# First weight slabs in four pieces with the squares held to their order, the last branch product moved behind the gate tiles, and own areas for the last two tiles

## The chip, the cores and the metric

The kernel runs on one core of one Trainium2 chip. The metric is the device time of one execution in microseconds (us). Numbers of the trace come from one profiled execution, counted from its first instruction.

## The reference, cut to what matters

One step of a decoder layer is computed for 512 prompt tokens and 8 times 4 sample tokens, 544 in all, in float32.

```
n = RMSNorm(h);  z = n @ W_in            # q | k | v | gate | u | v2 | gA | gB
branch A: retention per head (4 heads) -> group RMS norm -> * silu(gate)
branch B: gv = LayerNorm(gelu(v2));  yB = gelu(u) * (W_s[g] gv + b[g])
h += (sigmoid(gA) * (yA @ W_br_a) + sigmoid(gB) * (yB @ W_br_b)) @ W_o
h += relu(RMSNorm(h) @ W_up)^2 @ W_down
h += sigmoid(RMSNorm(h) @ W_pg) * (p @ W_pp)
y = RMSNorm(h)
```

W_s is lower triangular in chunks of 128 tokens. Outputs besides y are the retention states and the layer norm's result for the sample tokens.

## The kernel before, in words

Activations lie transposed: a tile is 128 features by 544 tokens, in one of 62 (later 69, then 74) **slots**, taken with `get()` from a first-in-first-out list and given back with `put()`. Each float32 operand is split into a high and a low part: `split` rounds on ScalarE (ACT, L124) and takes the rest on VectorE (DVE, L125). A product is three matmuls (high-high, high-low, low-high) on each half of 272 tokens, so one 128x128 block of weights costs six matmuls and one output tile over 1024 features 48 (`tile_of`, `dense`, L290). Large later products use a scheme with seven block products instead of eight (`fast_run`, L376).

**Feed.** Weights come in slabs of 128x1024 float32 (512 KB). `Feed.load` issues their DMAs on SyncE's queue (SP) into few raw buffers; `fill` splits them into few `hl` buffers ahead of use; `take` hands one over. For the fast scheme some sums of slabs are made by an accumulating DMA on GpSimd's queue (POOL) and on DVE (L226, L227).

**Order.** Python traces the instructions in program order; `later(n, fn)` and `chores` put work n ticks ahead, and `dense` ticks every second block. A scheduler with a simulated clock then orders each engine's queue: an instruction whose operands look ready may go ahead of earlier ones that wait. On the chip every queue runs in that fixed order. `pin`, which the change uses, ties an instruction behind the one traced before it on its engine.

**Start.** L544 to L555 load the eight input tiles x0 to x7; each is scaled and split (`scaled_split`, L481 on ACT, L482 on DVE). The first two slabs (both columns of q of head 0) come in two pieces each, slab 0 behind x0 and slab 1 behind x4. `first_two` then runs both q tiles block by block. `start_norm` squares the eight tiles (L454, L457), adds them up (L458), and `inverse_rms` sums over features with a matmul of ones (L470), then root (L473, ACT) and reciprocal (L475, DVE). `normalise` (L607), `times_r1` (L584) and `rotary` on DVE need that reciprocal.

**Middle.** Behind head 3 come the eight tiles of the gMLP's v2, m = 0 to 7 (`tiles_in`, gelu on ACT, L969; then transposed by `gated_by_token`, L956 to L962). Between m = 3 and m = 4 the PSUM pools are changed and `branch_a(3)` runs (eight products, added to the sum on DVE, L643). `x_operands` makes the operands of the fast scheme (L980 and L318 to L327) in four chores. In the run that follows, in the fast scheme (gelu of u, the gelu run), chores make the statistics (L1018), the `moments` (root on ACT, L1024, which needs another function table than gelu) and the `layer_norm` (ten DVE instructions, L1054). Tiny ACT copies (`after`, L990) hold back the loads of `wst`, `bs` and `wss`, the spatial weights. `spatial` (L1086 to L1107) runs in the next such run, that of sigmoid(gA).

**End.** The last stage runs half by half of the tokens: `gate_tiles` gives two W_pg tiles of 272 tokens one PSUM area (`two_banks`, one tile in each bank), which is read at L1320, or, for the very last pair, one tile at a time at L1326: times the norm's factor, sigmoid (L1327), times the embedding (L1330), added to h (L1331), squared (L1333, L1335). The very last tile goes in two pieces of 136 tokens. L1329 is a tiny root that fetches ACT's root table early. `finish` then makes the last norm (L470, L473, L475), scales (L1370, L1373) and stores.

Of the kernel before, what the change touches and what calls it, by code (L numbers as in the profile page):

```python
# [9 lines left out]
F32R = mybir.dt.float32r  # L10
# [4 lines left out]
P = 128  # L15
# [23 lines left out]
FIRST = (0, 4)  # L39
# [48 lines left out]
def layer(tc, a, o):  # L88
    nc = tc.nc
    act, dve, pool, pe = nc.scalar, nc.vector, nc.gpsimd, nc.tensor  # L90
    with ExitStack() as ctx:
# [35 lines left out]
        class Feed:  # L127
# [26 lines left out]
            def load(self, pieces=1):  # L154
                while self.jobs:
# [12 lines left out]
                    for i in range(pieces):  # L168
                        c = slice(i * SLAB // pieces, (i + 1) * SLAB // pieces)
                        nc.sync.dma_start(t[:, c], srcs[0][:, c])  # L170
                    self.loaded.append((kind, [t]))
                    if pieces > 1:
                        return
# [18 lines left out]
            def wide(self, src, pieces=1):  # L192
                pool_, n = self.hl_turn[0]
                self.hl_turn.rotate(-1)
                t = pool_.tile([P, 2 * SLAB], F32R, tag="hl", name="hl", bufs=n)
                for i in range(pieces):
                    c, d = (slice(i * SLAB // pieces + e, (i + 1) * SLAB // pieces + e) for e in (0, SLAB))
                    split(t[:, c], t[:, d], src[:, c])
                return [(t[:, :SLAB], t[:, SLAB:])]
# [14 lines left out]
            def expand(self, kind, tiles):  # L214
# [23 lines left out]
                return [("wide", lambda: done(self.wide(tiles[0], 2 if kind == "halves" else 1), 1))]  # L238
# [213 lines left out]
        def add_square(total, src, first):  # L452
            if first:
                act.activation(total, src, AF.Square)  # L454
            else:
                t = get()
                act.activation(t, src, AF.Square)  # L457
                dve.tensor_tensor(out=total, in0=total, in1=t, op=ALU.add)  # L458
                put(t)
# [31 lines left out]
        for h in range(H):  # L491
            for i in range(12):
                feed.plan("halves" if h == 0 and i < 2 else "plain", a["w_in"][12 * h + i])
# [49 lines left out]

        xs_raw, xs = [], []  # L544
        for k in range(KD):
# [25 lines left out]
        def start_norm():  # L571
            total = get()
            for k in range(KD):
                add_square(total, xs_raw[k], k == 0)
# [413 lines left out]
        def after(t, x):  # L988

            act.copy(t[:1, :1], x[:1, :1])  # L990

        def spatial_weights(x):
            after(wst[:, 0], x)
            nc.sync.dma_start(wst, a["wsT"])
# [5 lines left out]
        def sample_weights(x):  # L1000
            after(bs[:, 0], x)
            nc.sync.dma_start(bs, a["bs"])
            after(wss[:, 0, 0], x)
            nc.sync.dma_start(wss, a["wsS"])
# [9 lines left out]
        def statistics(i):  # L1014

            for j in range(5):
                n = P if j < 4 else NS
                dve.bn_stats(out=stats[:n, j, i], in_=gvt[j][i][:n, :512])  # L1018

        def moments():  # L1020
# [3 lines left out]
            act.activation(mv[:, :, 1], mv[:, :, 1], AF.Sqrt, bias=eps, scale=1.0)  # L1024
            dve.reciprocal(mv[:, :, 1], mv[:, :, 1])

        for m in range(0, KD, 2):
            if m == 4:
# [14 lines left out]
                branch_a(before.h, before.ya)  # L1043
                chores([(1 + 4 * k, x_operands, k) for k in range(4)])
            for i, t in enumerate(tiles_in(AF.Gelu)):
                later(2 * i + 2, lambda m=m + i, t=t: gated_by_token(m, t))
            if m == 4:
                later(2, lambda: statistics(0))

        def layer_norm(j):  # L1050
            n = P if j < 4 else NS
            for i in range(2):
                x = gvt[j][i][:n, :512]
                dve.tensor_scalar(  # L1054
                    out=x, in0=x, scalar1=mv[:n, j, 0:1], scalar2=mv[:n, j, 1:2], op0=ALU.subtract, op1=ALU.mult
                )
# [11 lines left out]

        us = []
        chores([(7, statistics, 1), (9, moments)] + [(12 + 3 * j, layer_norm, j) for j in range(5)])  # L1070
        later(26, sample_gates)
        for u2 in fast_run([(x_ops, AF.Gelu)] * 4):
# [412 lines left out]
```

## Time and profile before

| | us |
|---|---|
| median of 3 runs | 1270.65 (1269.56 to 1272.1) |
| the profiled execution's own time | 1270.25 |
| its span from first to last instruction | 1268.3 |
| TensorE busy in it | 1241.2 (98%) |
| DVE, ACT, GpSimd busy | 886.2, 625.4, 92.8 |

The 1.95 us between the span and the execution's own time lie outside what the trace records. Busy time of TensorE is modelled from the starts of pipelined matmuls, so a busy TensorE can still run slowly; how many matmuls a stretch holds tells more.

### The profile page before, as it was taken

The page shows a single profiled execution, that of the slowest core. Times are in us where ns is not written, and L with a number is a line of the kernel's source. Part 1 is how long each engine was busy: PE and PEld are TensorE (multiplying, and loading weights), DVE is VectorE, ACT ScalarE, POOL GpSimd, SP SyncE. Part 2 cuts the span into 40 slices and gives each one's busy share as a digit, 9 for nine tenths or more (in the row PEclk, how much of TensorE's full clock was granted, in tenths as well). Part 3 has the DMA queues.
Part 4 walks back from the last instruction along what each step waited for, and adds up shares of the span by engine and source line. Part 5 has one row for each costly group of instructions (what it writes and reads, how often), then busy time and mean ns, then how long its engine had stood idle before and what let it go on. Part 6 is the DMA issues. An engine that isn't in the chain of part 4 may idle for free.

```text
span 1268.3 us, 22931 instructions
## 1 busy us (share of the span) xinstructions
PE 1241.2 (98%) x9432; PEld 1209.1 (95%) x9432; DVE 886.2 (70%) x1293; ACT 625.4 (49%) x1044; POOL 92.8 (7%) x127
## 2 busy tenths in 40 slices
PE   9999999999999999999899999999999999999995
PEld 8989999999999998999899999999999999999995
DVE  7976853696468645864778654559359889878966
ACT  6454553344434443623545532445248558577732
POOL 0211100110010001000110000000000000000000
PEclk9999999999999999999999999999999999999998
DMA  8228223722273226543654552223546667755302
GB/s 323 98 99 272 98 83 112 277 82 88 98 261 106 67 92 221 172 137 78 188 142 127 158 202 93 89 79 99 118 125 159 173 164 186 186 153 146 117 18 71
DMA packets 64760, 176.27 MB, mean 139 GB/s; under 512 B 7344, under 2 KB 9648, under 8 KB 64656
## 3 DMA queue, kind: packets, MB, share of 16 engines
q1 hardware_dynamic: 53712, 135.42, 32.1%
q0 software_dynamic: 10944, 39.39, 13.3%
q8 instruction: 74, 1.21, 0.4%
q14 instruction: 30, 0.25, 0.1%
HBM read 153.55 MB, written 21.23 MB: 138 GB/s over the span
## 4 chain that ended last, share of the span: by engine, by line
PE 90%; DVE 5%; ACT 2%; DMA 1%; issue 1%; POOL 0%; SPq 0%; DVEq 0%; ACTq 0%
PE f L290 48%; PE fa L376 15%; PE f L376 11%; PE pg L290 4%; PE o L450 2%; PE st L450 2%; DVE hl L125 2%; PE sc L450 1%; PE su L813 1%; PE so L810 1%; PE so L811 1%; ACT hl L124 1%; DVE s L125 1%; PE norm L470 1%; PE sp L1086 1%
## 5 line engine op out<-in xcount | busy, mean ns | idle before, releaser
L290 PE MATMUL f<-s,hl 128*128 128x272 f32 x5088 | 674.6, 290 | 3.7 <-DVE s L482 0.9
L290 PEld LDWEIGHTS f<-s,hl 128*128 128x128 f32 x5088 | 655.4, 188 | 12.2 <-DVE s L482 1.6
L125 DVE TENSOR_TENSOR hl<-raw,hl 128x1024 fp32r<-128x1024 f32 (+1 forms) x255 | 288.4, 1138 | 114.3 <-ACT hl L124 110.9
L124 ACT CAST hl<-raw 128x1024 fp32r<-128x1024 f32 (+1 forms) x255 | 248.3, 980 | 179.3 <-PE f L290 108.5
L376 PE MATMUL fa<-s,hl 128*128 128x272 f32 x1728 | 241.3, 290 | 5.4 <-ACT hl L124 4.3
L376 PEld LDWEIGHTS fa<-s,hl 128*128 128x128 f32 x1728 | 225.2, 189 | 8.2 <-ACT hl L124 5.2
L376 PE MATMUL f<-s,hl 128*128 128x272 f32 x1296 | 184.7, 290 | 2.9 <-DVE s L395 1.1
L376 PEld LDWEIGHTS f<-s,hl 128*128 128x128 f32 x1296 | 171.1, 189 | 4.8 <-DVE s L395 2.0
L124 ACT CAST s<-s 128x544 fp32r<-128x544 f32 (+4 forms) x170 | 97.2, 597 | 51.9 <-DVE s L319 12.5
L125 DVE TENSOR_TENSOR s<-s,s 128x544 fp32r<-128x544 f32 (+4 forms) x170 | 108.0, 656 | 6.2 <-ACT s L124 5.6
L814 DVE SCALAR_TENSOR_TENSOR state<-state,su 128x512 f32<-128x512 f32 x64 | 43.6, 684 | 37.8 <-PE su L813 37.7
L125 DVE TENSOR_TENSOR s<-state,s 128x512 fp32r<-128x512 f32 x64 | 42.7, 686 | 20.2 <-ACT s L124 17.2
L124 ACT CAST s<-state 128x512 fp32r<-128x512 f32 x64 | 37.8, 620 | 38.5 <-DMA state<-in_state 20.0
L403 ACT ACTIVATE s<-fa 128x272 f32<-128x272 f32 x36 | 14.3, 397 | 62.1 <-PE fa L376 62.1
L590 ACT COPY s<-f 128x544 f32<-128x544 f32 x28 | 17.2, 614 | 50.1 <-PE f L290 50.0
L475 DVE RECIPROCAL s<-s 128x544 f32<-128x544 f32 (+1 forms) x9 | 28.6, 3173 | 9.6 <-ACT s L473 9.6
L180 POOL DMA_DIRECT2D raw<-in_w_up x12 | 10.4, 864 | 306.8 <-DVE s L125 186.8
L643 DVE TENSOR_TENSOR s<-s,f 128x544 f32<-128x544 f32 x24 | 17.2, 716 | 19.8 <-PE f L290 19.8
L290 PE MATMUL pg<-s,s 128*128 128x272 f32 x240 | 30.7, 288 | 0.0
L290 PEld LDWEIGHTS pg<-s,s 128*128 128x128 f32 x240 | 30.3, 188 | 0.1
L818 POOL DMA_DIRECT2D out_state_s<-state x32 | 22.9, 716 | 101.0 <-DVE state L814 101.0
L450 PE MATMUL o<-s,vh 128*128 128x256 f32 (+2 forms) x128 | 30.3, 323 | 0.0
(183 smaller groups left out, 1125.0 us busy)
## 6 DMA issues: line engine op xcount, KB each, us to landing
raw<-in_w_in SPq DMA_DIRECT2D x66, 512.0 KB, 3.3
state<-in_state SPq DMA_DIRECT2D x32, 512.0 KB, 4.7
out_state_s<-state POOLq DMA_DIRECT2D x32, 512.0 KB, 4.5
raw<-in_w_in SPq DMA_DIRECT2D x40, 256.0 KB, 3.2
raw<-in_w_up SPq DMA_DIRECT2D x20, 512.0 KB, 3.3
raw<-in_w_down SPq DMA_DIRECT2D x20, 512.0 KB, 3.3
raw<-in_w_up SPq DMA_DIRECT2D x36, 256.0 KB, 3.1
raw<-in_w_down SPq DMA_DIRECT2D x36, 256.0 KB, 3.3
```

The costliest lines, as they stand in the source:

```text
L124: act.copy(hi, src)
L125: dve.tensor_tensor(out=lo, in0=src, in1=hi.bitcast(F32), op=ALU.subtract)
L290: pe.matmul(ps.p[s], w, x[:, s * TH : (s + 1) * TH], start=first and i == 0 and j == 0, stop=last and i == n - 1 and j == 2, skip_group_ch ...
L376: pe.matmul(ps, a_, b_, start=first and k == j == 0, stop=k == 3 and j == 2, skip_group_check=True)
L403: act.activation(t1[:, hi_half], pa, AF.Copy, scale=-1.0)
L450: pe.matmul(ps[:rows, c], u, v, start=i == 0 and j == 0, stop=i == n - 1 and j == 2)
L470: pe.matmul(ps, ones, t[:, c0 - at0 : c1 - at0], start=i == 0, stop=i == len(totals) - 1)
L475: dve.reciprocal(r[:, c], r[:, c])
L590: act.copy(halves(t), ps.all)
L643: dve.tensor_tensor(out=halves(acc_a[m]), in0=halves(acc_a[m]), in1=ps.all, op=ALU.add)
L814: dve.scalar_tensor_tensor(out=raw[:, i], in0=raw[:, i], scalar=gamma**LS, in1=ps, op0=ALU.mult, op1=ALU.add)
L818: pool.dma_start(o["state_s"][b, c.h].rearrange("(i p) v -> p i v", i=2), raw)
```

## The change

**At the start** both first slabs are begun together and come in four pieces of 256 columns (128 KB each), a piece of both behind x0, x2, x4 and x6, split as they come. The squares and their sum are traced behind that loop and pinned there.

**In the middle** all eight v2 tiles come ahead of `branch_a(3)`, whose slabs are also loaded later. The first statistics are spread over the tiles m = 6 and 7, the second ones, the moments and the layer norm over `branch_a(3)`, pinned in the order of tracing. The loads of the spatial weights are pinned on SP behind what was traced there, in place of the ACT copies. `spatial` runs two at a time behind each pair of the gelu run.

**At the end** the last two tiles of the second half get an area of two banks each, and L1326 reads the second tile from its own.

```
+        feed.begin(2)
...
-            if k in FIRST:
-                feed.load(2)
-            if k == 1:
-                feed.fill(1)
-            if k == FIRST[1] + 1:
-                feed.fill(2)
+            if k % 2 == 0:
+                feed.piece(k // 2)
+        total = get()
+        for k in range(KD):
+            add_square(total, xs_raw[k], k == 0, pin)
...
+            def begin(self, n):
+                self.first = []
+                for _ in range(n):
+                    _, srcs = self.jobs.popleft()
+                    hl = self.hl()
+                    self.first.append((self.raw(), hl, srcs[0]))
+                    self.parts.append(("wide", [(hl[:, :SLAB], hl[:, SLAB:])]))
+            def piece(self, i):
+                c, d = (slice(i * SLAB // 4 + e, (i + 1) * SLAB // 4 + e) for e in (0, SLAB))
+                for t, hl, src in self.first:
+                    nc.sync.dma_start(t[:, c], src[:, c])
+                for t, hl, src in self.first:
+                    split(hl[:, c], hl[:, d], t[:, c])
...
         for i in range(48, 56):
             feed.plan("plain", a["w_in"][i])
-            if i == 51:
-                plan_branch_a(H - 1)
+        plan_branch_a(H - 1)
...
-                branch_a(before.h, before.ya)
                 chores([(1 + 4 * k, x_operands, k) for k in range(4)])
+                spatial_weights()
...
             if m == 4:
-                later(2, lambda: statistics(0))
+                chores([(3 + 2 * j, statistics, 0, j) for j in range(5)])
...
-        chores([(7, statistics, 1), (9, moments)] + [(12 + 3 * j, layer_norm, j) for j in range(5)])
-        later(26, sample_gates)
+        sample_weights()
+        chores([(5 + j // 2, statistics, 1, j) for j in range(5)] + [(8, moments)])
+        chores([(9 + j, layer_norm, j) for j in range(5)])
+        branch_a(before.h, before.ya)
+        later(6, sample_gates)
+        us = []
         for u2 in fast_run([(x_ops, AF.Gelu)] * 4):
             us += u2
-            if len(us) == 2:
-                spatial_weights(us[0])
-            if len(us) == 4:
-                sample_weights(us[2])
+            chores([(1 + 3 * i, spatial, len(us) - 2 + i) for i in range(2)])
-        chores([(1 + 3 * m, spatial, m) for m in range(KD)])
...
+                elif s and i == KD - 2:
+                    todo = [*gate_tiles(s, ms[:1]), *gate_tiles(s, ms[1:])]
...
-                            dve.tensor_tensor(out=t1[:, p], in0=area[:, j, p], in1=r3[:, c], op=ALU.mult)
+                            ps = todo[0] if j else area
+                            dve.tensor_tensor(out=t1[:, p], in0=ps[:, 0, p], in1=r3[:, c], op=ALU.mult)
```

## Rows read from the trace of the kernel before

**Rows 1.** The page: busy us of each engine (share of the span) and instructions, then the shares of the span along the chain that ended last.
```profile
PE 1241.2 (98%) x9432; PEld 1209.1 (95%) x9432; DVE 886.2 (70%) x1293; ACT 625.4 (49%) x1044; POOL 92.8 (7%) x127
PE 90%; DVE 5%; ACT 2%; DMA 1%; issue 1%; POOL 0%; SPq 0%; DVEq 0%; ACTq 0%
```

**Rows 2.** Busy time by stretch: from:to, its us, then busy us (and instructions) of PE, PEld, DVE, ACT and POOL, the granted TensorE clock (1.00 is full), the DMA engines' share, GB/s.
```profile
22.90:60.00 37.10, 35.98 (x283) 35.11 (x281) 36.30 (x49) 18.23 (x29) 7.79 (x7) 1.00 0.44 164
845.00:925.00 80.00, 80.00 (x637) 79.96 (x636) 56.66 (x81) 34.69 (x50) 2.59 (x3) 1.00 0.38 106
```

**Rows 3.** The chain that ended last, in order of time, in the first 62 us: start, us, what.
```profile
2.67 4.96 DMA s<-in_xT
...
12.52 0.52 ACT hl L124
...
13.08 9.23 PE f L290 x70
22.31 0.93 PE norm L470 x4
...
24.89 1.22 DVE hl L125
26.11 3.48 DVE s L475
...
51.37 0.65 DVE s L584
```

**Rows 4.** Groups by line and shape in the first 23 us: busy us, mean ns of one, and the idle time before them with what ended it.
```profile
L482 DVE SCALAR_TENSOR_TENSOR s<-s,gcols,s 128x544 fp32r<-128x544 f32 x8 | 6.2, 781 | 4.1 <-ACT s L481 4.0
L481 ACT ACTIVATE s<-s,gcols 128x544 fp32r<-128x544 f32 x8 | 5.9, 740 | 2.0 <-DMA s<-in_xT 2.0
L458 DVE TENSOR_TENSOR s<-s,s 128x544 f32<-128x544 f32 x7 | 5.0, 719 | 0.0
L457 ACT ACTIVATE s<-s 128x544 f32<-128x544 f32 x7 | 4.5, 643 | 0.0
L125 DVE TENSOR_TENSOR hl<-raw,hl 128x512 fp32r<-128x512 f32 x4 | 2.7, 688 | 1.1 <-ACT hl L124 1.1
L124 ACT CAST hl<-raw 128x512 fp32r<-128x512 f32 x4 | 2.3, 610 | 0.9 <-DMA raw<-in_w_in 0.9
L124 ACT CAST hl<-raw 128x1024 fp32r<-128x1024 f32 x2 | 2.1, 1048 | 2.7 <-DMA raw<-in_w_in 2.7
L125 DVE TENSOR_TENSOR hl<-raw,hl 128x1024 fp32r<-128x1024 f32 x1 | 1.2, 1224 | 1.9 <-ACT hl L124 1.9
```

**Rows 5.** SyncE's queue in the first 60 us: two of its waits (us in total, times, longest), then three of its issues in order of time.
```profile
SPq L565 <- DMA s<-in_xT: 1.1, 3, 0.4
SPq L170 <- DMA s<-in_sin: 0.3, 1, 0.3
...
8.37 0.33 SPq L557 DMA_DIRECT2D s<-in_cos  x1
...
13.29 0.45 SPq L653 DMA_DIRECT2D dtab<-in_dtab  x1
...
14.76 1.29 SPq L170 DMA_DIRECT2D raw<-in_w_in  x3
```

**Rows 6.** The timeline of ACT, DVE and PE from 19 to 23 us: start, us, engine, line, what, and in brackets the idle time before and what ended it.
```profile
19.85 1.05 ACT L124 CAST hl<-raw 128x1024 fp32r<-128x1024 f32 x1 [2.73 <-DMA raw<-in_w_in]
20.93 1.22 DVE L125 TENSOR_TENSOR hl<-raw,hl 128x1024 fp32r<-128x1024 f32 x1 [1.88 <-ACT hl L124]
...
22.86 18.48 PE L290 MATMUL f<-s,hl 128*128 128x272 f32 x144
```

**Rows 7.** The timeline around the moments and the layer norm (columns as in rows 6).
```profile
602.90 1.28 ACT L1024 ACT_TABLE_LOAD   x1
...
604.75 4.64 DVE L1054 TENSOR_SCALAR s<-s,mv 128x512 f32<-128x512 f32 x10
...
606.39 1.28 ACT L414 ACT_TABLE_LOAD   x1
...
609.59 0.52 PE L376 MATMUL fa<-s,hl 128*128 128x272 f32 x2 [2.64 <-ACT hl L124]
...
610.59 2.28 PE L376 MATMUL fa<-s,hl 128*128 128x272 f32 x10 [0.47 <-DVE hl L125]
```

**Rows 8.** Busy time by stretch (columns as in rows 2): `branch_a(3)`, the tiles m = 4 to 7, the stall, two pieces of it, and a stretch with `spatial`.
```profile
538.60:563.80 25.20, 25.20 (x201) 25.18 (x202) 16.93 (x24) 6.89 (x16) 2.85 (x4) 1.00 0.50 126
563.80:589.10 25.30, 25.30 (x204) 25.28 (x203) 11.26 (x15) 8.50 (x19) 0.86 (x1) 1.00 0.41 122
605.40:614.90 9.50, 5.96 (x30) 5.21 (x29) 9.50 (x16) 5.34 (x9) 1.09 (x1) 0.82 0.66 151
609.50:610.60 1.10, 0.54 (x3) 0.32 (x3) 1.10 (x2) 0.04 (x1) 0.00 (x0) 1.00 0.76 104
611.50:612.50 1.00, 1.00 (x7) 1.00 (x6) 1.00 (x2) 0.60 (x2) 0.00 (x0) 0.50 1.02 234
625.00:674.00 49.00, 49.00 (x385) 48.00 (x384) 35.18 (x51) 23.76 (x39) 6.32 (x6) 1.00 0.65 165
```

**Rows 9.** The timeline where the PSUM pools change, and one line's instructions (ns least, median, most; first and last start).
```profile
538.58 3.28 PE L290 MATMUL f<-s,hl 128*128 128x272 f32 x24 [0.71 <-ACT s L969]
...
L980 DVE SCALAR_TENSOR_TENSOR s<-s,gcols,s x8: 776/785/786, 507.3 to 567.0; 128x544 f32<-128x544 f32 x8
```

**Rows 10.** The timeline of the end (columns as in rows 6).
```profile
1233.45 1.09 PE L470 MATMUL norm<-s,ones 128*128 128x136 f32 x8
...
1252.59 0.85 DVE L1326 TENSOR_TENSOR s<-pg,s 128x272 f32<-128x272 f32 x3 [1.34 <-PE pg L290]
1253.06 0.84 ACT L1327 ACTIVATE s<-s 128x272 f32<-128x272 f32 x3 [2.64 <-DVE s L1326]
...
1253.92 1.28 ACT L1329 ACT_TABLE_LOAD   x1
...
1255.45 0.30 DVE L1330 TENSOR_TENSOR s<-s,s 128x136 f32<-128x136 f32 x1 [0.92 <-ACT warm L1329]
1255.67 0.50 DVE L1331 TENSOR_TENSOR s<-s,s 128x136 f32<-128x136 f32 x2
...
1256.30 0.43 DVE L1346 TENSOR_TENSOR s<-s,s 128x272 f32<-128x272 f32 x1
...
1256.88 2.15 PE L470 MATMUL norm<-s,ones 128*128 128x136 f32 x8 [4.33 <-DVE s L1346]
```

More of the change, by code (lines that the diff above doesn't have):

```diff
@@ L38 @@
 WARM = 12
-FIRST = (0, 4)
 QK = ((7, 8, 9, 10), (0, 2, 4, 7))
@@ L152, in raw, with load @@
                 return pool_.tile([P, SLAB], F32, tag="raw", name="raw", bufs=n)
-            def load(self, pieces=1):
+            def begin(self, n):
[11 more added lines that the diff above has]
+                    split(hl[:, c], hl[:, d], t[:, c])
+                if i == 3:
+                    self.busy -= len(self.first)
+            def load(self):
                 while self.jobs:
@@ L167, in load @@
                     t = self.raw()
-                    for i in range(pieces):
-                        c = slice(i * SLAB // pieces, (i + 1) * SLAB // pieces)
-                        nc.sync.dma_start(t[:, c], srcs[0][:, c])
+                    nc.sync.dma_start(t, srcs[0])
                     self.loaded.append((kind, [t]))
-                    if pieces > 1:
-                        return
             def load_sums(self, s0, s1):
@@ L190, in load_pair, with hl, wide @@
                 return v, t, w
-            def wide(self, src, pieces=1):
+            def hl(self):
                 pool_, n = self.hl_turn[0]
                 self.hl_turn.rotate(-1)
[L195 to L198, printed above, removed]
+                return pool_.tile([P, 2 * SLAB], F32R, tag="hl", name="hl", bufs=n)
+            def wide(self, src):
+                t = self.hl()
+                split(t[:, :SLAB], t[:, SLAB:], src)
                 return [(t[:, :SLAB], t[:, SLAB:])]
@@ L237, in expand @@
                     return [("slots", lambda: done(self.stay(tiles[0]), 1))]
-                return [("wide", lambda: done(self.wide(tiles[0], 2 if kind == "halves" else 1), 1))]
+                return [("wide", lambda: done(self.wide(tiles[0]), 1))]
             def fill(self, n, **held):
@@ L492, in layer @@
             for i in range(12):
-                feed.plan("halves" if h == 0 and i < 2 else "plain", a["w_in"][12 * h + i])
+                feed.plan("plain", a["w_in"][12 * h + i])
                 if h and i == 3:
@@ L986, in x_operands, with spatial_weights @@
                 put(r1s["r"])
[L988 to L994, printed above, removed]
+        def spatial_weights():
+            pin(nc.sync.dma_start(wst, a["wsT"]))
             pool.affine_select(
@@ L998, in spatial_weights, with sample_weights @@
             )
[L1000 to L1004, printed above, removed]
+        def sample_weights():
+            pin(nc.sync.dma_start(bs, a["bs"]))
+            pin(nc.sync.dma_start(wss, a["wsS"]))
             pool.affine_select(
@@ L1012, in sample_weights, with statistics @@
             )
[L1014 to L1018, printed above, removed]
+        def statistics(i, j):
+            n = P if j < 4 else NS
+            pin(dve.bn_stats(out=stats[:n, j, i], in_=gvt[j][i][:n, :512]))
         def moments():
```

23 lines of the change are left out of this document (10 added, 13 removed).

## The prediction

> **What bounds the kernel now.** I read the page's busy times and chain first: TensorE is busy 98% of the span and makes 90% of the chain [rows 1]. So the time is the number of matmuls at full rate plus TensorE's gaps and slow stretches. The rate comes from an undisturbed stretch: 637 matmuls in 80.00 us, 0.126 us each [rows 2]. Then I read the busy times by stretch for where TensorE falls short; the change touches three such places.
>
> *The start.* The chain [rows 3] runs from the input tiles over ACT to the split of slab 1 at 12.52; only then, at 13.08, does TensorE run without gaps, to the end of the q tiles at 22.31. Behind them comes the norm's matmul, a slab's split on DVE (24.89), the reciprocal (26.11, 3.48 us), and from there a chain of DVE instructions to 51.37. From 22.9 to 60 DVE is busy 36.30 of 37.10 us [rows 2]: the reader is to see that this stretch belongs to DVE, and that what TensorE gains ahead of it counts only as far as DVE gets its work earlier.
>
> *The middle.* At 602.90 ACT fetches the root's table, at 606.39 it fetches gelu's again, and DVE does ten layer norm instructions from 604.75, 4.64 us [rows 7]. The splits of slabs queue behind both; TensorE waits 2.64 us for one. Two further things are to be seen in [rows 8]: from 605.40 to 614.90, 9.50 us, TensorE does 30 matmuls, and the clock granted is full (2.4 GHz) until 610.60 and half (1.2 GHz) from 611.50, after the gap.
>
> *The end.* The first reading of the last pair's area starts at 1252.59, as the last matmul ends, and covers three pieces [rows 10]: the whole first tile and both pieces of the second. DVE idled 1.34 us before it. The tail then waits for the table (1.28 us) before it can overwrite what L1329 reads, so L1330 idles 0.92 us.
>
> **The change part by part.** The sum is made against the profiled execution's 1270.25 us; the median of the runs is 0.40 us above that.
>
> *Start.* ACT loses the eight squares between scalings (8 x 0.64 = 5.1 us). Its four casts of 512 columns (0.610 us each) become eight of 256; from 0.610 and 1.048 us for 512 and 1024 columns, 256 take 0.39, together 3.1 in place of 2.4 [rows 4]. On DVE 256 columns take 0.42 from 0.688 and 1.224, 3.4 in place of 2.7, and the seven additions (5.0) move behind the loop. The x tiles arrive as before: SP's queue waits for earlier transfers to land [rows 5], in order the issue eight places on starts as one lands, so cos at 8.37 and dtab at 13.29 mark x2 and x7 landed at about 8.3 and 13.2. Ahead of x7 lie the same bytes after the change. x7 is scaled and split by 13.2 + 0.74 + 0.78, about 14.8. TensorE has both slabs' first quarter from about 6.5, needs 12 matmuls (1.51 us) per x tile, waits for x1 until about 8.4 and then has every tile in time: 8.4 + 7 x 1.51 less the part of x1's matmuls that runs before its low part, about 18.8. That is 3.5 us ahead of 22.31.
>
> What is late next: slab 2. Its issue waits for sin to land, at 14.76 [rows 5], bytes ahead of it being the same, and its cast starts at 19.85 after 2.73 us of waiting for that DMA [rows 6]. So the k tiles can start at 20.9 with the high part and run on from 22.15, against 22.86: TensorE keeps about 1.2 of the 3.5 us. The norm fits in the gap: the squares end near 14 + 8 x 0.6 = 18.8 on ACT, the additions near 19.5. DVE then has slabs 2, 3 and 4 (3 x 1.14) and the reciprocal (3.48) from 20.93 on, 27.8 at the earliest, against 26.11 + 3.48 = 29.6 before, in whichever order they are queued. Bounds: nothing (the queue's order keeps the reciprocal late) and 3.5 us (all of TensorE's lead). I take 1.6, nearer to the DVE chain of [rows 3], which ends last there.
>
> The Trainium skill speaks against this part. "DMA: Bandwidth & Descriptors", section "Rules for kernel authors", wants small transfers joined into large ones. The trace has no 128 KB weight piece; it shows 272 KB tiles landing 0.7 us apart with eight in flight. By the page the start would lose; by the rows it loses nothing. What it would do here is a rival below.
>
> *Middle.* The stretch from 605.40 to 614.90 holds 30 matmuls, 3.8 us at 0.126; 5.7 us are lost [rows 8]. The change takes the moments and the layer norm to `branch_a(3)`. What comes there: DVE 4.64 for the layer norm and about 3.5 for the second statistics and moments, ACT one table and one root, 1.6 us; the way back to gelu's table falls in the first pair of the gelu run (1.28). The cover: at its present place that product leaves DVE idle 8.27 of 25.20 us and ACT 18.31 [rows 8], and its slabs of 48 matmuls (6 us) are split up to three ahead, where the gelu run used four split slabs per 12 us. If the cover is gone, the 5.7 us come back there. `spatial` (some 1.6 us of DVE each) now goes two to a pair through the gelu run; in its present stretch, eight in 49 us, TensorE is busy throughout and DVE 35.18 [rows 8], and the gelu run loses over 8 us of DVE work to the move. I cost it at nothing. On SP the three pinned loads come ahead of slab loads; on POOL the selects precede the accumulating loads. Both queues are nearly empty there (POOL 2.85 of 25.20) and what waits behind them has several slabs' time. The three ACT copies (0.2 us each) go. The wait of 0.71 us at the change of PSUM pools [rows 9] stays, with another product behind it. Bounds: 0 and 5.7; I take 5.7, as the idle rows at the new place are nearer to full cover.
>
> *End.* The first tile's multiply, sigmoid and the rest can run while TensorE does the last 24 matmuls (3.0 us). Left behind 1252.59: two multiplies and two sigmoids, so the table load starts 0.36 + 0.27 earlier, about 0.6; and behind the table only L1330, L1331 and one square of the last piece, where a second L1331 (0.21), the addition of squares L1346 (0.36) and one order gap fall away, 0.7 [rows 10]. Together 1.3, at least 0.9. The norm's matmuls then start 3.0 us behind the last ones in place of 4.33; they take 2.15 at the half clock here and 1.09 at the full clock in the first half [rows 10]. In the middle the clock was still full as matmuls came back after 2.64 us, and half about 1 us later [rows 8]. So 0 to 1.06; I take 0.5. "TensorE: Matmul & The Clock Gate" of the Trainium skill, section "Part 1: The HAM clock gate", says that recent activity sets the clock; those rows agree.
>
> **Sum.** 1.6 + 5.7 + 1.3 + 0.5 = 9.1 us; 1270.25 - 9.1 = 1261.15, and with part of the distance to the median 1261.3.
>
> **The rivals.**
>
> *A: the layer norm's stall only moves*, because DVE in the new place also has x operands left over, each 2 x 0.785 for L980 [rows 9] and some 3 us more. For: DVE was busy 16.93 of 25.20 us there. Against: the split slabs ahead. Without the 5.7: 1270.25 - 3.4 = 1266.9.
>
> *B: small pieces stretch the stream.* Four transfers more ahead of x7 and sin; if each costs one 0.7 us step as the tiles do [rows 5], slab 2 comes 2.8 us later, the k tiles too: the start goes from -1.6 to +1.2, 1263.9 in all. It would not turn the sign; with A it would give 1269.6, no change. This is what the page's rule on small transfers amounts to here. Against: SP's waits end with bytes landed.
>
> *C: the last pair's pieces still wait together.* Were L1326 queued or waiting as before, 1.8 us are gone: 1263.0. For: the trace shows an idle DVE, not why; against: two tiles share an area now, and nothing else was due.
>
> *D, slower: slots.* `branch_a(3)`'s eight operands hold their slots 24 us longer. Of 69, by the code, up to 66 are then taken (xs 16, sums 8, operands 8, gelu tiles 10, x operands 16 and those in work), so the gelu of m = 4 to 7 takes slots that x operands have just left, and queues behind 4.7 us of DVE work. Four such waits less the cover of two other PSUM areas (6 us) are 12.8, and the time 1274. It decides from 2.9 us of wait per tile, 11.6 in all. For: the count; against: DVE and ACT are half idle from 563.80 to 589.10 [rows 8].
>
> **How the numbers follow.** Forecast 0.60, A 0.13, B 0.10, C 0.06, D 0.07, A with B 0.04. The forecast alone spans its bounds: 1270.25 less (3.5 + 5.7 + 1.3 + 1.06) is 1258.7, and with 0 at the start and 0.9 at the end 1263.7. The range has to take A's 1266.9 in to leave out no more than 2 in 10: 1258 to 1267.3. About 0.2%, 2.5 us, is what a measurement of this kernel can tell from no change. Faster: forecast, B, C and A, less a part of each for two of them together, 0.83. Same: 0.09. Slower: D and what I have not seen, 0.08.
>
> **What would show it.** Start right: q tiles end before 19.5, slab 2's cast still near 19.9, the reciprocal ends before 28.5; wrong: TensorE held before the k tiles beyond 22.2. Middle right: no wait of TensorE over 1 us and no half clock from 580 to 665, the root's table fetched while `branch_a(3)` runs; wrong: a gap there, or gelu L969 waiting on DVE in m = 4 to 7 (D). End right: the first tile's L1326 starts about 3 us before the last matmul ends, and the norm's matmul some 3.0 us behind it. The prediction falls if the scheduler's new order puts a long DVE instruction ahead of a split that TensorE needs, anywhere.

## The result, and the profile after

| | before | after |
|---|---|---|
| median, us | 1270.71 (4 runs) | 1261.93 (4 runs, 1260.18 to 1263.26) |
| profiled execution, its own time | 1270.25 | 1260.18 |
| its span | 1268.3 | 1258.4 |

The ratio is 0.993, 95% interval 0.9912 to 0.9947: 8.9 us less, between 6.7 and 11.2. Forecast were 1261.3 us, and 1258.0 to 1267.3 as the range. The profiled execution of after is the fastest of its four, so its trace shows more gain (9.9 us of span) than the medians do.

The changed kernel has other line numbers: L290 is now L304, L376 L390, L124 and L125 are L123 and L124, L458 L474, L470 L486, L473 L489, L475 L491, L1054 L1058, and the end's L1326 to L1333 are L1332 to L1339. First the page of the kernel after, the lines that answer to [rows 1]: busy times, and the chain's shares.

```profile
PE 1236.8 (98%) x9432; PEld 1206.0 (96%) x9432; DVE 887.0 (70%) x1297; ACT 630.3 (50%) x1047; POOL 92.6 (7%) x127
...
PE 53%; DVE 2%; ACT 2%; DMA 1%; issue 0%; DVEq 0%; ACTq 0%
```

TensorE still sets the end. (The chain of after could be followed back only to 520.85 us, so its shares sum to about half of the span and can't be set beside those of before.) The 9.9 us can be placed by following one instruction through both traces. Two rows of the chain of the kernel before, the norm and the first group of the fast scheme behind it:

```profile
844.44 0.92 PE norm L470 x4
...
929.84 1.50 PE fa L376 x12
```

The same two of the chain of the kernel after:

```profile
838.64 0.92 PE norm L486 x4
...
923.92 1.49 PE fa L390 x12
```

And from its timeline the norm of the first half, which stands at 1233.45 in [rows 10]:

```profile
1225.79 1.09 PE L486 MATMUL norm<-s,ones 128*128 128x136 f32 x8
```

The lead is 5.9 us at 930 us and 7.7 at the first half's norm (1233.45 less 1225.79). At 510 us, ahead of the middle, it is -0.2: the last matmul group of the heads starts at 511.50 before and at 511.73 after. So the start lost 0.2 us, the middle won 6.1, a stretch between 930 and 1225 us that no part of the change touches won 1.7, and the end the rest, some 2.2.

**The start** of the kernel after, its timeline (start, us, engine, line, what, and in brackets the idle time before and what ended it):

```profile
18.75 0.59 ACT L602 COPY s<-f 128x544 f32<-128x544 f32 x1
19.83 1.04 ACT L123 CAST hl<-raw 128x1024 fp32r<-128x1024 f32 x1 [0.48 <-DMA raw<-in_w_in]
...
20.91 1.23 DVE L124 TENSOR_TENSOR hl<-raw,hl 128x1024 fp32r<-128x1024 f32 x1 [0.44 <-ACT hl L123]
...
20.93 0.77 PE L304 MATMUL f<-s,hl 128*128 128x272 f32 x4 [1.61 <-ACT hl L123]
...
22.05 0.72 DVE L474 TENSOR_TENSOR s<-s,s 128x544 f32<-128x544 f32 x1
...
22.19 3.17 PE L304 MATMUL f<-s,hl 128*128 128x272 f32 x23 [0.49 <-DVE hl L124]
...
25.19 1.08 PE L486 MATMUL norm<-s,ones 128*128 128x272 f32 x4
...
26.83 3.56 DVE L491 RECIPROCAL s<-s 128x544 f32<-128x544 f32 x1 [1.27 <-ACT s L489]
```

The reciprocal in the same view of the kernel before (the chain of [rows 3] has its start at 26.11):

```profile
26.03 3.54 DVE L475 RECIPROCAL s<-s 128x544 f32<-128x544 f32 x1
```

TensorE is through with the q tiles near 19.3 instead of 22.31, then waits 1.61 us for slab 2 and has the k tiles earlier than before. Yet the reciprocal, from which the DVE chain of [rows 3] runs on, starts at 26.83 instead of 26.03. The row at 22.05 tells why: it is the last of the seven additions of squares, and it stands in DVE's queue behind slab 2's split of 20.91. So the norm's matmul can't run in TensorE's gap; it comes behind the 27 first matmuls of the k tiles, at 25.19.

The transfers did not stay where they were. SyncE's queue in the kernel after has these two issues, at 13.29 and 14.76 before [rows 5]:

```profile
13.78 0.58 SPq L665 DMA_DIRECT2D dtab<-in_dtab  x1
...
15.88 1.86 SPq L185 DMA_DIRECT2D raw<-in_w_in  x4
```

By the prediction's own marks, x7 landed about 0.5 us later and slab 2 was issued 1.1 us later. In this execution slab 2 was ready for its cast at the old time all the same.

**The middle**, busy time by stretch of the kernel after (columns as in [rows 2]): the two stretches of the gate tiles and `branch_a(3)`, which have changed places, and the former stall.

```profile
538.60:563.80 25.20, 24.92 (x200) 24.88 (x201) 16.54 (x25) 11.48 (x32) 5.80 (x6) 1.00 0.55 156
563.80:589.10 25.30, 25.30 (x204) 25.28 (x203) 18.12 (x33) 7.98 (x17) 0.88 (x1) 1.00 0.42 100
605.40:614.90 9.50, 9.50 (x77) 9.34 (x76) 7.41 (x11) 4.24 (x8) 0.00 (x0) 1.00 0.67 187
```

From 605.40 to 614.90 there are 77 matmuls where [rows 8] has 30; 47 at 0.126 us are 5.9 us. The root's table and the layer norm now stand here (one row of the timeline, then one line's instructions with the ns least, median, most and the first and last start):

```profile
579.79 1.28 ACT L1028 ACT_TABLE_LOAD   x1
```

```profile
L1058 DVE TENSOR_SCALAR s<-s,mv x10: 527/542/545, 582.1 to 589.9; 128x512 f32<-128x512 f32 x8, 32x512 f32<-32x512 f32 x2
```

TensorE does 204 matmuls in that stretch, as many as in the second of [rows 8], at the full clock. The ten layer norm instructions no longer come in one piece of 4.64 us but in groups of two, four and four, with slab splits between; whether the new place or the grouping covers them no run here separates. Its longest wait from 500 to 670 us (in total, times, longest) is the one at the change of PSUM pools, which was 0.71 before [rows 9]:

```profile
PE f L304 <- ACT s L981: 0.8, 1, 0.8
```

**The end**, timeline of the kernel after:

```profile
1240.74 4.15 PE L304 MATMUL pg<-s,s 128*128 128x272 f32 x32
...
1241.94 0.44 DVE L1332 TENSOR_TENSOR s<-pg,s 128x272 f32<-128x272 f32 x1
...
1244.93 0.51 DVE L1332 TENSOR_TENSOR s<-pg,s 128x136 f32<-128x136 f32 x2 [0.65 <-PE pg L304]
...
1245.80 1.28 ACT L1335 ACT_TABLE_LOAD   x1
...
1247.33 0.30 DVE L1336 TENSOR_TENSOR s<-s,s 128x136 f32<-128x136 f32 x1 [1.01 <-ACT warm L1335]
...
1247.90 1.04 PE L486 MATMUL norm<-s,ones 128*128 128x136 f32 x6 [1.50 <-DVE s L1339]
```

The first tile is read at 1241.94, 3 us ahead of the last matmul's end (1244.89); only the two pieces of the second remain behind it. The last six norm matmuls start 3.0 us behind the last W_pg matmul and take 1.04 us at the full clock, where eight took 2.15 at the half clock [rows 10]. One wait is left: L1336 still idles 1.01 us until the table is there.

### The profile page after: what moved, and what is told of

It is laid out like the page before. It is cut to its first block, busy times and chain, and to the rows that moved or that the text cites. A ratio compares the mean times of both kernels' runs of the same rounds, so it can differ in the third digit from the quotient of the medians.

```text
span 1258.4 us, 22939 instructions
## 1 busy us (share of the span) xinstructions
PE 1236.8 (98%) x9432; PEld 1206.0 (96%) x9432; DVE 887.0 (70%) x1297; ACT 630.3 (50%) x1047; POOL 92.6 (7%) x127
## 4 chain that ended last, share of the span: by engine, by line
PE 53%; DVE 2%; ACT 2%; DMA 1%; issue 0%; DVEq 0%; ACTq 0%
PE f L304 20%; PE fa L390 16%; PE f L390 12%; PE pg L304 4%; DVE hl L124 1%; PE sp L1081 1%; ACT hl L123 1%; DMA raw<-in_w_down 0%; PE norm L486 0%; DVE s L491 0%; DVE s L124 0%; DMA raw<-in_w_pg 0%; PE sp L1082 0%; PE gt L968 0%; DVE s L880 0%
## 5 line engine op out<-in xcount | busy, mean ns | idle before, releaser
L304 PE MATMUL f<-s,hl 128*128 128x272 f32 x5088 | 674.0, 289 | 4.5 <-ACT hl L123 1.8
L304 PEld LDWEIGHTS f<-s,hl 128*128 128x128 f32 x5088 | 655.2, 188 | 12.5 <-ACT hl L123 2.2
L124 DVE TENSOR_TENSOR hl<-raw,hl 128x1024 fp32r<-128x1024 f32 (+2 forms) x259 | 288.8, 1123 | 107.3 <-ACT hl L123 105.1
L123 ACT CAST hl<-raw 128x1024 fp32r<-128x1024 f32 (+2 forms) x259 | 249.1, 969 | 177.2 <-PE f L304 99.0
L390 PE MATMUL fa<-s,hl 128*128 128x272 f32 x1728 | 238.9, 289 | 2.0 <-ACT hl L123 1.0
L390 PEld LDWEIGHTS fa<-s,hl 128*128 128x128 f32 x1728 | 224.3, 188 | 4.2 <-ACT hl L123 1.6
L390 PE MATMUL f<-s,hl 128*128 128x272 f32 x1296 | 183.5, 288 | 1.7 <-DVE s L409 1.1
L390 PEld LDWEIGHTS f<-s,hl 128*128 128x128 f32 x1296 | 170.1, 188 | 3.1 <-DVE s L409 2.0
L123 ACT CAST s<-s 128x544 fp32r<-128x544 f32 (+4 forms) x170 | 97.4, 598 | 48.0 <-DVE s L765 12.2
L124 DVE TENSOR_TENSOR s<-s,s 128x544 fp32r<-128x544 f32 (+4 forms) x170 | 108.6, 659 | 6.4 <-ACT s L123 5.7
L123 ACT CAST s<-state 128x512 fp32r<-128x512 f32 x64 | 37.9, 621 | 38.4 <-DMA state<-in_state 18.7
L124 DVE TENSOR_TENSOR s<-state,s 128x512 fp32r<-128x512 f32 x64 | 42.8, 687 | 19.8 <-ACT s L123 16.7
L491 DVE RECIPROCAL s<-s 128x544 f32<-128x544 f32 (+1 forms) x9 | 28.6, 3176 | 10.0 <-ACT s L489 10.0
L304 PE MATMUL pg<-s,s 128*128 128x272 f32 x240 | 30.7, 288 | 0.0
L804 ACT ACTIVATE km<-k,maskb 96x256 fp32r<-96x256 f32 x32 | 15.9, 508 | 29.3 <-PE su L825 28.6
L304 PEld LDWEIGHTS pg<-s,s 128*128 128x128 f32 x240 | 30.3, 188 | 0.1
```

The costliest lines, as they stand in the source:

```text
L123: act.copy(hi, src)
L124: dve.tensor_tensor(out=lo, in0=src, in1=hi.bitcast(F32), op=ALU.subtract)
L304: pe.matmul(ps.p[s], w, x[:, s * TH : (s + 1) * TH], start=first and i == 0 and j == 0, stop=last and i == n - 1 and j == 2, skip_group_ch ...
L390: pe.matmul(ps, a_, b_, start=first and k == j == 0, stop=k == 3 and j == 2, skip_group_check=True)
L491: dve.reciprocal(r[:, c], r[:, c])
L804: act.activation(km, c.k3.bitcast(F32), AF.Copy, scale=maskb[:, b : b + 1])
```

## The experiments

Ratios are to the kernel before on the same chip, with the 95% interval behind them; differences in us are the ratio's distance from 1 times the median of before there, which lay between 1268.69 and 1270.17.

### Each part alone

`s_only`: the kernel before with the start's parts of the edit (`begin`, `piece`, the pinned squares).

> The kernel before with the start's part alone. Theory (as the two traces read): the q tiles end some 3 us earlier, but the last addition of the squares stands behind slab 2's split on DVE, the reciprocal starts no earlier than at 26.0, and the time stays within 1 us of 1270.7. Rival (the prediction's term): the reciprocal's end comes forward and the time is 1.6 us lower, 1269.1. A third: the four pieces make slab 2 late and the time rises by over 1 us.

Measured 1271.04, ratio 1.0014 (1.0002 to 1.0025): slower by 1.8 us, between 0.3 and 3.2. The trace repeats that of the whole change: slab 2's issue at 15.85 and its cast at 19.87, k tiles from 20.97, the last addition at 22.09, the reciprocal at 26.87. It does not show where the 1.8 us lie: its execution took 1270.02 us, the third fastest of twelve. A half clock behind the gap, as in `a_warm` below, would fit and is not shown here. The expected third case (late pieces, over 1 us more) has the size and not, in this trace, the late cast.

`m_only`: the kernel before with the middle's parts of the edit.

> The kernel before with the middle's part alone. Theory: the stall around the layer norm goes with its half clock, 5.7 to 6.2 us off 1270.7, so 1264.5 to 1265.0, and TensorE waits nowhere over 1 us between 515 and 740 us. Rival: part of what the whole change gained comes from how start and middle act together, and alone the middle gives 4 us or less.

Measured 1263.05, ratio 0.9948 (0.9936 to 0.9961): 6.6 us less, between 5.0 and 8.1; 77 matmuls in the former stall, as in the whole change.

`e_only`: the kernel before with the end's parts of the edit.

> The kernel before with own areas for the last two tiles alone. Theory: the stretch from the last W_pg matmul to the end of the norm's matmuls shrinks from 6.5 to about 4.1 us, of which about 1 us is the norm's matmuls at the full clock; time 2.2 to 2.4 us lower, 1268.4. Rival: the norm still runs at the half clock here and the gain is 1.3 us, 1269.4.

Measured 1267.74, ratio 0.9983 (0.9973 to 0.9993): 2.2 us less, between 0.9 and 3.4. Its norm at the end, timeline:

```profile
1254.93 1.73 PE L470 MATMUL norm<-s,ones 128*128 128x136 f32 x6 [1.50 <-DVE s L1336]
```

These six came at the half clock (1.73 us for six), behind the same idle 1.50 us that left the clock full in the kernel after. So the clock there goes either way from one execution to another. The gain is the one expected with the full clock, the clock in this execution that of the rival.

By medians (1271.04, 1263.05 and 1267.74 against 1270.17) the parts sum to -8.7 us (0.87 - 7.12 - 2.43), and the whole change measures -8.8 by its own. By the ratios they sum to 1.8 - 6.6 - 2.2 = -7.0 against -8.9 (6.7 to 11.2), with intervals of some 1.5 us to either side on each part. So nothing shows that they help or hinder each other, though 1 or 2 us of it could not be seen.

### What made the stall in the middle

Two causes were named together in the prediction: ACT's fetches of tables for the root, and ten layer norm instructions on DVE. They are taken out one at a time, from the kernel before.

```
-            act.activation(mv[:, :, 1], mv[:, :, 1], AF.Sqrt, bias=eps, scale=1.0)
+            act.activation(mv[:, :, 1], mv[:, :, 1], AF.Copy, scale=1.0)
```

`b_noroot` (the root of the moments is left out):

> The kernel before; the root of the layer norm's moments is replaced by a copy, so that the variance itself is used and ACT fetches no other table there. Left out: the root. Theory: the stall at 605 to 615 us comes from ACT and DVE one behind the other (two table fetches of 1.28 us, then 4.64 us of layer norm on DVE), so without the fetches a part of some 3 us goes and the gap may get too short for the clock to fall; 1266 to 1267.5. Rival one: ACT's fetches were the whole of it, 1264.5. Rival two: DVE's layer norm alone was it, no change, 1270.

Measured 1268.99, ratio 0.9995 (0.9984 to 1.0005): no change that shows, and at most 2 us less. The theory's 3 us did not come; the time is that of the second rival. TensorE's two waits there, in its timeline:

```profile
603.04 4.64 DVE L1054 TENSOR_SCALAR s<-s,mv 128x512 f32<-128x512 f32 x10
...
606.79 0.52 PE L376 MATMUL fa<-s,hl 128*128 128x272 f32 x2 [1.06 <-ACT hl L124]
...
608.87 2.63 PE L376 MATMUL fa<-s,hl 128*128 128x272 f32 x10 [1.57 <-DVE hl L125]
...
611.30 2.92 PE L376 MATMUL f<-s,hl 128*128 128x272 f32 x12
```

The longer wait is now for DVE's half of the split, behind the 4.64 us of layer norm, and the clock falls as before (2.92 us for twelve). From 605.40 to 614.90 there are 31 matmuls, against 30 before.

```
-        chores([(7, statistics, 1), (9, moments)] + [(12 + 3 * j, layer_norm, j) for j in range(5)])
+        chores([(7, statistics, 1), (9, moments)])
```

`b_noln` (the ten layer norm instructions are left out):

> The kernel before with the ten layer norm instructions on DVE left out (the results that rest on them are wrong; the root and both table fetches stay). If DVE's 4.64 us in one piece make the stall, the stretch from 605 to 615 us is nearly full, TensorE has no wait over 1 us and no half clock there, and the time falls by 4 to 6 us (ratio 0.996). If the two table fetches on ACT make a stall of their own, a wait of 1 us or more for a slab's cast stays near 608 us and the gain is under 3 us (ratio 0.998 or more).

Measured 1269.14, ratio 0.9996 (0.9984 to 1.0008): no change again, and at most 2 us less. Its timeline:

```profile
603.95 1.28 ACT L1024 ACT_TABLE_LOAD   x1
...
605.56 1.28 ACT L414 ACT_TABLE_LOAD   x1
606.86 0.40 ACT L414 ACTIVATE s<-fa 128x272 f32<-128x272 f32 x1
607.15 3.45 ACT L124 CAST hl<-raw 128x512 fp32r<-128x512 f32 x4
...
608.76 0.52 PE L376 MATMUL fa<-s,hl 128*128 128x272 f32 x2 [2.75 <-ACT hl L124]
...
612.53 2.57 PE L376 MATMUL f<-s,hl 128*128 128x272 f32 x12
```

Without the DVE work the casts stand behind both table fetches, and TensorE waits 2.75 us, no less than before; the window of the stall holds 33 matmuls. The first of my two theories (DVE's work alone makes the stall) fell here, as that of the tables alone had fallen with `b_noroot`. What was left was that each is enough by itself. `b_neither` takes both out:

> The kernel before with both left out: the moments' root is a copy and the ten layer norm instructions on DVE are gone (the results that rest on them are wrong). Leaving out either one alone gave no change (0.9995 and 0.9996). If ACT's two table fetches and DVE's layer norm are each long enough to hold the slab's split alone, and the stall is the later of the two, then without both it is gone: no wait of TensorE over 1 us and the full clock from 600 to 620 us, 60 or more matmuls from 605.4 to 614.9 us in place of 30, and 4 to 6 us less, ratio 0.995 to 0.997. If the stall has a third cause (the slabs' landing, or the work of that place as such), a wait over 1 us stays and the ratio is 0.998 to 1.001.

Measured 1264.17, ratio 0.9955 (0.9941 to 0.9968): 5.7 us less (4.1 to 7.5), most or all of the stall. The former stall by windows, and TensorE's waits from 500 to 670 us (in total, times, longest):

```profile
605.40:614.90 9.50, 8.96 (x67) 8.53 (x68) 6.74 (x8) 5.56 (x10) 0.88 (x1) 1.00 0.80 213
```

```profile
PE f L290 <- ACT s L969: 0.7, 1, 0.7
PE fa L376 <- ACT hl L124: 0.4, 1, 0.4
```

The window holds 67 matmuls at the full clock, where 30 were before and 77 after the change. From the start of the norm behind the heads (517.57 before) to that of the next one (844.28; 844.44 in the chain above), `b_neither`'s trace is 4.3 us shorter than the kernel before's; the eight traces with the middle's part are 5.9 to 6.1 us shorter. One reservation: the scheduler orders the queues anew in each of these kernels (the sample gates' instructions at L1063 start at 613.96 before and at 601.70 in `b_noln`), so what is left out is not all that differs.

### Mending the start

`a_early` issues slabs 2 and 3 right behind x7; `a_order` pins slab 2's split on DVE behind the last addition, and the first matmul of the k tiles behind the norm's; `a_both` does both. All start from the changed kernel.

```
+        feed.load()
         cos, sin = get(), get()
```

> The changed kernel; slabs 2 and 3 are issued right behind x7, ahead of the cosine and the other tables. Theory: slab 2's landing (19.83 us in the changed kernel's trace, 20.91 in the one with the pinned root) holds the first k tile after a gap of 1.6 to 3.0 us, in which the clock can fall; landing near 16 it is split right behind the squares, the gap goes, and the last addition behind that split comes about 1 us earlier, so the reciprocal starts near 24 in place of 26.8 and the time is 2 to 3 us lower, 1259 to 1260. Rival: DVE's chain to 52 us is set by the order of its queue alone, the reciprocal stays past 26 and the gain is under 0.5 us.

Measured 1261.24, ratio 0.9937 (0.9923 to 0.9952). The cast came 0.6 us sooner, but the k tiles did not: a q tile's copy in ACT's queue held them (below), the last addition again stood behind slab 2's split (22.03), and the reciprocal came at 27.84, as the rival has it. The k tiles in its timeline:

```profile
20.85 1.07 PE L304 MATMUL f<-s,hl 128*128 128x272 f32 x4 [1.93 <-ACT s L603]
...
22.17 4.19 PE L304 MATMUL f<-s,hl 128*128 128x272 f32 x23 [0.25 <-DVE hl L124]
```

23 matmuls took 4.19 us here and 3.17 in the kernel after: the clock was granted at 0.71 on average from 22.2 to 26.2, behind a gap of 1.93 us in place of 1.61.

```
-            dve.tensor_tensor(out=lo, in0=src, in1=hi.bitcast(F32), op=ALU.subtract)
+            order(dve.tensor_tensor(out=lo, in0=src, in1=hi.bitcast(F32), op=ALU.subtract))
...
+                        if hold:
+                            hold.pop()
+                            tc.keep_in_program_order(ins)
```

> The changed kernel; slab 2's split on DVE is pinned behind the last addition of the squares, and the first k matmul behind the norm's matmuls on TensorE. Slab 2 lands as late as before. Theory: the norm's sum is then ready near 20.3 in place of 22.8, but the root stands behind the cast of slab 4 on ACT, so the reciprocal starts near 25, 1.5 us earlier; 1260.4. Rival: the landing of slabs 2 to 4 decides alone and the time stays at 1261.9.

Measured 1261.53, ratio 0.9938 (0.9923 to 0.9952). The norm's matmul did come in the gap, at 22.37, but in this execution slab 2's cast waited for its DMA until 22.72, the granted clock was 0.74 on average from 21 to 27 us, and the reciprocal came at 27.58.

> Both of the last two edits. Theory: the reciprocal starts near 23.5 and the gap ahead of the k tiles is under 1 us: 3 us lower than the changed kernel, 1259. Rival: one of the two does all there is, and both together give no more than it.

Measured 1262.36, ratio 0.9939 (0.9926 to 0.9953). In its profiled execution the start runs as the prediction had it:

```profile
21.85 1.18 PE L495 MATMUL norm<-s,ones 128*128 128x272 f32 x4 [2.11 <-DVE s L483]
...
22.67 7.54 PE L310 MATMUL f<-s,hl 128*128 128x272 f32 x57
...
25.12 3.54 DVE L500 RECIPROCAL s<-s 128x544 f32<-128x544 f32 x1
```

TensorE waits 2.11 us for the norm's sum; behind it the k tiles run without a gap at the full clock, and the reciprocal is 1.7 us earlier than in the kernel after. Its median shows nothing of that; the interval is 3.4 us wide, so a gain of 1 us can't be excluded, and neither can none.

### The table at the end

`a_warm`: the changed kernel, but the early root reads a constant instead of the tile, so that nothing that writes the tile waits for it; it is pinned behind the last sigmoid.

```
-                                act.activation(warm, t1[:, TH - 1 : TH], AF.Sqrt)
+                                pin(act.activation(warm, eps, AF.Sqrt))
```

> The changed kernel; the tiny root that fetches ACT's table early reads a constant and is pinned behind the last sigmoid, where it read the last sigmoid's output. Theory: in the changed kernel the last piece's multiply waits 1.01 us for that root's reading (it overwrites what is read); without it the multiply starts right behind the last sigmoid, and the norm's matmuls about 1.3 us earlier, 1260.6 against the changed kernel's 1261.9. Rival: the root needs the table anyway, so the fetch stays last on the path and the gain is under 0.4 us.

Measured 1262.22, ratio 0.9938 (0.9924 to 0.9952), no better than the changed kernel. In its trace the end did shrink: the last six norm matmuls idle 0.49 us instead of 1.50, and from the last W_pg matmul's end to the root it is 3.0 us against 4.1. The profiled execution lost it again at the start:

```profile
20.91 1.04 ACT L123 CAST hl<-raw 128x1024 fp32r<-128x1024 f32 x1 [1.35 <-DMA raw<-in_w_in]
...
22.00 0.77 PE L304 MATMUL f<-s,hl 128*128 128x272 f32 x4 [3.04 <-ACT hl L123]
...
23.26 4.44 PE L304 MATMUL f<-s,hl 128*128 128x272 f32 x23 [0.49 <-DVE hl L124]
```

Nothing of the start differs in the two kernels, yet slab 2's cast came 1.1 us later, TensorE's gap was 3.04 us, the granted clock 0.50 from 24 to 26 us, and the reciprocal at 29.18.

### Two versions to follow from it

`me_warm` leaves the start as before and takes the middle, the end and the constant root; `best1` takes all parts with all the repairs above.

> The start as before, the middle and the end as changed, and the early fetch of the root's table no longer reading the tile (pinned behind the last sigmoid). If the parts add up as they did alone (middle -6.6, end -2.2 us) and the pinned fetch gives its 1.1 us of the tail, the time is 9.9 us below the kernel before: ratio 0.992, some 1.5 us below the changed kernel. If the start's part does not really cost anything and its loss alone was chance, it is level with the version that has all parts and the pinned fetch: ratio 0.994. In the trace: k tiles start near 22.9 us and the reciprocal near 26.1; no wait of TensorE over 1 us from 545 to 665 us; 3.0 us from the last W_pg matmul to the final root.

Measured 1259.61, ratio 0.9926 (0.9911 to 0.9942): 9.4 us less, where 9.9 were expected if the parts add up.

> The changed kernel with the early issue of slabs 2 and 3, slab 2's split behind the last addition, the first k matmul behind the norm's, and the pinned fetch of the root's table. If the start's repair and the fetch add up (some 1 us each below the changed kernel at 0.993), the ratio is 0.991 to 0.992. If the repair of the start is lost in the variation of the slabs' landing, as the runs with one or two of these edits suggest, it is 0.993 to 0.994, and the version with the old start is at least as good.

Measured 1259.41, ratio 0.9928 (0.9914 to 0.9942): 9.1 us less, which does not decide between the two cases. Both are well ahead of the kernel before. Their intervals hold the changed kernel's 0.993 too, so that they beat it is likely by the traces (a tail 1.1 us shorter) and not shown by the times. In the trace of `me_warm` the old start is whole, with the k tiles at 22.56, and the tail short:

```profile
22.56 8.67 PE L290 MATMUL f<-s,hl 128*128 128x272 f32 x66
...
25.73 3.55 DVE L477 RECIPROCAL s<-s 128x544 f32<-128x544 f32 x1
...
1248.53 0.96 PE L472 MATMUL norm<-s,ones 128*128 128x136 f32 x6 [0.49 <-DVE s L1328]
```

What each start is worth can be read in every trace from two instructions: the reciprocal, and the first matmuls of the next norm, behind the four heads. That norm in the kernel before, and in the kernel after:

```profile
517.57 0.62 PE L470 MATMUL norm<-s,ones 128*128 128x272 f32 x2
```

```profile
517.80 0.62 PE L486 MATMUL norm<-s,ones 128*128 128x272 f32 x2
```

| start | traces | reciprocal starts, us | that norm starts, us |
|---|---|---|---|
| as before | `before`, `m_only`, `e_only`, `b_noroot`, `b_noln`, `b_neither`, `me_warm` | 25.39 to 26.47 | 516.99 to 518.01 |
| as changed | `after`, `s_only`, `a_warm` | 26.83, 26.87, 29.18 | 517.80, 517.64, 520.08 |
| one repair | `a_early`, `a_order` | 27.84, 27.58 | 518.61, 519.43 |
| both repairs | `a_both`, `best1` | 25.12, 24.88 | 516.98, 516.71 |

From the one to the other every trace takes 490.8 to 491.9 us, so what the reciprocal wins or loses is still there behind the heads, to within 1.1 us. The changed start wins nothing in any of its three traces; with both repairs it is level with the best of the old ones. Each row is one execution. The clock shows a second price: none of the seven traces with the old start has a half clock between 14 and 600 us, while four of the seven with a new one have it right behind the gap ahead of the k tiles (`a_early`, `a_order`, `a_warm` and `best1`, a granted clock of 0.72 to 0.74 on average from 21 to 27 us).

## Why the prediction was right, and where it was not

The time was right within 0.6 us of the median, but one term of the sum had the wrong sign and others made up for it, so that closeness is in part luck.

**Start: a gain of 1.6 forecast, a loss of 0.2 in the trace, and of 1.8 us (0.3 to 3.2) for the part alone.** TensorE's side of the step held: the q tiles end ahead of 19.5 and the k tiles start at 20.93. On the DMA side only the end held in this execution, with slab 2's cast at 19.83 against 19.85; its issue, which the prediction left at 14.76 because the bytes ahead are the same, came at 15.88. The step that failed is "DVE then has slabs 2, 3 and 4 and the reciprocal from 20.93 on, 27.8 at the earliest ... in whichever order they are queued", and the one before it, that the additions end near 19.5 and the norm fits in the gap. Six additions ran until 20.46, one behind the other at 0.81 us each, and the seventh stood behind slab 2's split. Seven in a row would by that rate have ended near 21.3, an estimate, behind the k tiles' start already: in `a_order` and `a_both`, where the order is mended, TensorE waits 2.6 and 2.1 us for the sum. But it was the order that carried the norm's matmul past TensorE's gap and behind 27 others. The sign I wrote down for a right start (reciprocal done before 28.5) shows it: it is done at 30.39. What the sum left out altogether is the price of a new gap: before, TensorE runs through to the k tiles; after the change it waits 1.6 to 3.0 us ahead of the k tiles, and in four of the seven traces with a new start the clock falls behind the wait; in two of them (`a_early`, `a_warm`) the same 23 matmuls take 1.0 and 1.3 us more. The prediction has TensorE run without gaps from 13.08 on, which is a link of the chain; in the timeline its last wait before that, 0.31 us, is over at 11.94.

**Middle: 5.7 forecast, 6.1 in the trace, 6.6 (5.0 to 8.1) alone.** The place, the size and the cover all held. The reading of the stall was too simple, though: I told it as one queue behind two works. `b_noroot`, `b_noln` and `b_neither` show two stalls lying on top of each other: leaving out only the root, or only the layer norm, gave nothing that shows (at most 2 us). That moving only one would have given as little follows from this and was not run. The change moves both.

**End: 1.3 and 0.5 forecast, 2.2 in the trace, 2.2 (0.9 to 3.4) alone.** The last norm matmuls start the forecast 3.0 us behind the last W_pg matmul. Under-sized was the rest: two of the eight norm matmuls now run while the table is fetched, so six remain at the end, and in this execution they came at the full clock, 1.04 us against 2.15, where the sum had taken 0.5. At the half clock (`e_only`) the six cost 0.7 us more. "TensorE: Matmul & The Clock Gate" of the Trainium skill, section "Part 1: The HAM clock gate", has recent activity set the clock; the rows agree in direction, but the same idle times gave both levels in two kernels.

**What was not forecast**: 1.7 us between 930 and 1225 us in the profiled execution. There, before, ACT's casts wait for an input tile's landing (1.73 us ahead of 1109.18 and 1.23 us ahead of 1111.05), and TensorE waits 0.83 us for a split ahead of 1119.31; after, that wait of TensorE is absent. It is not the change's: of the kernels with only a part of it, `m_only` has the wait (0.86 us ahead of 1113.29) and `e_only` has not. From the norm that starts at 844.28 before (844.44 in the chain above) to the next one, at 1208.49, the fourteen traces take from 362.4 to 365.5 us, 364.2 before and 362.4 after. The profiled execution of after is at the short end, 1.75 us below the median of its runs.

**The rivals.** A (the layer norm's stall only moves) fell: 204 matmuls in its new place, no wait over 0.8 us. B (small pieces stretch the stream) fell in its size of 2.8 us and is open in its direction: slab 2 is issued at 15.77 to 16.23 in the four traces with this order of loads (`after`, `s_only`, `a_warm`, `a_order`), against 14.27 to 15.06 in the seven with the old start, and its cast comes at 19.83, 19.87, 20.91 and 22.72 against 19.16 to 20.50. "DMA: Bandwidth & Descriptors" of the Trainium skill, section "Rules for kernel authors", wants small transfers joined; the later issue agrees in direction, but no run varies the size of the pieces alone. C (the last pair's pieces wait together) fell with the row at 1241.94. D (slots) fell: the gelu of the gate tiles waits only at the change of pools. None of the four names the order of one addition in DVE's queue, which kept the reciprocal late; the prediction's closing sentence, on a DVE instruction ahead of what TensorE needs, came nearest, with the roles reversed.

**Open**: why slab 2 is issued about 1 us later with the new start and lands at times 1 to 3 us later still, and how much a mended start is worth in the median; its effect is of the size of the variation.

## What to carry to other kernels

When a stall has two works in front of it on two engines, take out each alone and then both: if either is long enough, taking away one gives nothing that shows, and the change is worth its price only when it moves both. A lead won on one engine counts where the next chain begins: follow it instruction by instruction through the queue of the engine that carries that chain, and don't accept "in whichever order". A stretch that ran without a gap is worth something; a faster head that ends in a wait for the next slab can pay with the clock what it won.

## What the runs showed of the hardware

- The clock after a short gap isn't fixed by the gap's length. Ahead of the k tiles it stayed full behind 1.61 us (`after`, 23 matmuls in 3.17 us) and 1.97 us (`s_only`, 3.16), and it fell behind 1.93 us (`a_early`, 4.19) and 3.04 us (`a_warm`, 4.44); at the end, behind two gaps of 1.04 and 1.50 us, it was full in one kernel and half in another (1.04 and 1.73 us for the same six matmuls).
- Slab 2, behind the same transfers in the same queue, was ready for its cast at 19.83 in one execution (`after`) and at 20.91 in another (`a_warm`); a gain that hangs on the landing of one slab is of that size of uncertainty.
